# Storing two bias tables once instead of 128 times, reading them with a mirrored skew, and reading the mirrored tile backwards on VectorE

## The chip, the cores and the metric

The kernel runs on one core of a Trainium2 chip. The metric is the device time of one execution in microseconds (us). The times shown are those of three runs of the kernel before the change: 1046.44, 1047.62 and 1049.24 us, median 1047.62.

## What is computed

One layer of a hybrid decoder trunk on 512 tokens with 1024 features, in float32: a SwiGLU half-step, two kinds of attention side by side, their output projection, a second SwiGLU half-step, and a gated embedding. The change touches only how the relative-position bias of the attention reaches the softmax. Cut to that:

```python
def swiglu(x, w_gu, w_down):                 # 1024 -> 2 x 2816 -> 1024
    g, u = jnp.split(x @ w_gu, 2, axis=-1)
    return (jax.nn.silu(g) * u) @ w_down

def banded_attention(q, k, v, rel_bias, max_dist, stride):
    logits = einsum(q, k) * dh ** -0.5
    rel = query index - key index
    bias = rel_bias[t5_bucket(rel * stride)]         # one value per head and distance
    logits = where(0 <= rel <= max_dist, logits + bias, -1e30)
    m = max(logits); pr = exp(logits - m); s = sum(pr); o = pr @ v
    return o, m, s

h = h + 0.5 * rms(swiglu(rms(h), ffn1_w_gu, ffn1_w_down))
z = rms(h) @ w_in + b_in
out_a = sink_swa_gqa(...)       # 8 query heads, 2 key heads, window 128, a sink logit per head
out_b = dilated_mixture(...)    # 8 heads, (window, dilation) in (128,1), (512,4), (2048,16)
h = h + rms(concat(out_a, out_b) @ w_out + b_out)
h = h + 0.5 * rms(swiglu(rms(h), ffn2_w_gu, ffn2_w_down))
h = h + rms(sigmoid(rms(h) @ w_gate) * (p @ w_ple))
```

The bias depends on the head and on the distance between query and key alone. So a head's whole bias is a vector over distances, and the tile that is added to 128 queries by 512 keys is that vector, shifted by one element from one query to the next.

## The kernel before, in words

Every weight matrix is cut into tiles of 128 x 1024 values. A tile goes through the same steps each time (`prep`, L121): SyncE issues a DMA of 512 KB from DRAM into one of three raw buffers (L131), ScalarE casts it to float32r into a ring slot (L132), VectorE subtracts the cast from the raw values into the slot's second half (L133; on GpSimd in the attention), and TensorE multiplies with both halves, three products for each. `release` frees a slot when its last matmul is written down, and `pump` then starts the next tile. All DMAs of the kernel are issued by SyncE, in one order (queue "SPq"); an issue that waits holds all behind it.

The first SwiGLU walks over 22 slices of 128 features (`ffn`, L349). Each slice takes two weight tiles (gate and up, "gu"), 48 matmuls, a Silu on ScalarE (L250), a product on VectorE (L251) and a split into two halves (L252, L253). After slice 6 it calls `tables` (L402).

`tables` makes the bias vectors. Four small matmuls pick the bucket of each distance for 8 heads (L414), four VectorE adds put in the mask (L417). The result lies on 8 partitions of the buffer `FB`, 640 values for the dilated heads and 384 for the windowed ones. Then two DMAs (L421) store it in DRAM tiles `tbb` (8 x 128 x 640) and `tba` (8 x 128 x 384): each head's vector is written 128 times, by a step of 0 on the reading side. The same regions of `FB` are later taken for the three loads of the residual stream `x` that end the first SwiGLU (`load_h`, L198 to L200), which therefore wait for the two stores.

In the attention `load_tab` (L523) reads two heads' tables into SBUF, 128 partitions x 2 heads x 512 (or 256) values. Partition p reads copy p at an offset that goes down by one element from copy to copy (a step of 639 between rows of 640), so partition p holds the vector shifted by p, longest distance first.

`qk_b` (L580) and `qk_a` (L654) compute the logits of a head in four parts by query tile, and a custom VectorE instruction adds the table's slice to the logits in PSUM and takes the row's minimum of the negated, scaled sum (L595 and L674, followed by a short read of the accumulator). ScalarE exponentiates, VectorE scales (L601, L685), TensorE transposes and multiplies by V. Between the heads TensorE is given parts of the input and output projections to fill its time (`filling`, L754).

What matters of order: TensorE's order is the program's; the other engines' and SyncE's order is set by a scheduler that simulates the program, so a shorter DMA can change the order of SyncE's queue.

Of the kernel before, what the change touches and what calls it, by code (L numbers as in the profile page):

```python
# [30 lines left out]


def bias_constants():
    """Per table: which bucket each column (a distance, longest first) takes, times 8, and what is added."""
    b = _buckets(512)
    out = []
    for n, far in ((640, 511), (384, 255)):
        pick = np.zeros((32, n), np.float32)
        add = np.full((8, n), MASKED, np.float32)
        for r in range(n):  # L40
            d = far - r
            if n == 640:
                c = int(0 <= d <= 128) + int(d >= 0 and d % 4 == 0) + int(d >= 0 and d % 16 == 0)
            else:
                c = int(0 <= d <= 127)
            if c:
                pick[b[d], r] = 8.0
                add[:, r] = 8.0 * math.log(c)
        out += [pick, add]
    return out  # L50
# [3 lines left out]
def hybrid_layer(ctx: ExitStack, tc: tile.TileContext, x, p, rel_bias, ffn1_pre_g, ffn1_w_gu, ffn1_w_down,  # L54
# [28 lines left out]

    hd = tc.dram_tile([S, D], F32, name="hd")
    ed = tc.dram_tile([S, D], F32, name="ed")
    tbb = tc.dram_tile([8, P, 640], F32, name="tbb")
    tba = tc.dram_tile([8, P, 384], F32, name="tba")

    make_identity(nc, ident)
    nc.vector.memset(neghalf, -0.5)  # L90
# [10 lines left out]

    ring = [(WR[:, 2 * i, :], WR[:, 2 * i + 1, :]) for i in range(4)]

    # ---- weights: raw from DRAM, then the part that float32r holds and what is left of it
    W = {}
    state = {"raw": 0, "lo": nc.vector}

# [43 lines left out]
        return slot[0][:, k * P:(k + 1) * P], slot[1][:, k * P:(k + 1) * P]  # L151

    def wstat(o, slot, k, cols, start, stop):
        """o += W[k-th rows].T @ xT[k, cols]"""
        wh, wl = kview(slot, k)
        mm(o, wh, XH[:, k, cols], start, False)
        mm(o, wh, XL[:, k, cols], False, False)
        mm(o, wl, XH[:, k, cols], False, stop)

    def xstat(outs, ah, al, wh, wl, start, stop):  # L160
        """outs[n] += a.T @ W[:, n-th 512 columns]"""
        n = len(outs)
        for i in range(n):
            mm(outs[i], ah, wh[:, i * 512:(i + 1) * 512], start, False)
        for i in range(n):
            mm(outs[i], ah, wl[:, i * 512:(i + 1) * 512], False, False)
        for i in range(n):
            mm(outs[i], al, wh[:, i * 512:(i + 1) * 512], False, stop)
# [4 lines left out]
    def flat(a):  # L173
        return a.rearrange("p a b -> p (a b)")

    # ---- norms, one tile of 128 tokens at a time
    cnt = {"h": 0, "x": 0, "s": 0}

    def buf(kind):
# [8 lines left out]
        return small[:, i:i + 1]  # L188

    def rstd(src, junk, half):  # L190
        """1/sqrt(mean of squares + eps), halved if half"""
        ms, r = col(), col()
        nc.scalar.activation(junk, src, AF.Square, scale=1.0 / (16.0 if half else 32.0), accum_out=ms)  # L193
        nc.gpsimd.tensor_scalar(ms, ms, 4 * EPS if half else EPS, None, op0=ALU.add)  # L194
        nc.gpsimd.tensor_tensor(r, ms, neghalf, op=ALU.pow)
        return r
# [10 lines left out]
        return xs  # L207

    def post(t, f, gain, half, y, junk):
        """h + post-norm of f; y takes f * gain"""  # L210
        h = load_h(t, x if state.get("first") else None)
        with tc.high_priority():
            r = rstd(f, junk, half)
            nc.vector.tensor_tensor(y, f, gain, op=ALU.mult)
            nc.vector.scalar_tensor_tensor(h, y, r, h, op0=ALU.mult, op1=ALU.add)
        return h
# [17 lines left out]
        nc.sync.dma_start(BC[:, i, :n], dram(vec, off, [[0, P], [1, n]]))  # L234
        return BC[:, i, :n]

    # ---- SwiGLU
    def gu_half(ffn, ff, slot, cols):
        ps = slot2(slot)
        for i, kind in enumerate("gu"):  # L240
# [22 lines left out]
    halfA, halfB, full = slice(0, 256), slice(256, 512), slice(0, 512)  # L263
    HEAD_FF = 3

    # ---- order of the weights through the ring
    todo += [("ple", 0), ("ple", 1)]

    def gu_list(ffn):
# [1 line left out]

    todo += gu_list("1") + [("d1", k) for k in range(NFF)]

    # ---- start: e = p @ W_ple, first norms
    ring_more = [(ht(7), 11), (ht(8), 13), (ht(9), 15), (ht(10), 17)]
    free.extend(a for a, _ in ring_more[:3])
    praw = FB[:, 6144:7168].rearrange("p (k t c) -> p k t c", k=2, t=NT)
# [69 lines left out]
    release(("ple", 1))  # L347

    def ffn(n, wait_tr, after_first, extra_slots):  # L349
        """wait_tr(t): emits the transposition of token tile t"""  # L350
        wait_tr(0)
        wait_tr(1)
        for ff in range(HEAD_FF):
            gu_half(n, ff, gu_slot(ff), halfA)
            if ff < 2:
                wait_tr(2 + ff)
        for ff in range(NFF):
            s = gu_slot(ff)
            for slot, until in extra_slots:
                if ff == until:  # L360
                    retired.append(slot)
                    free[:] = [a for a in free if a is not slot]
            gu_half(n, ff, s, halfB if ff < HEAD_FF else full)
            gu_evac(n, ff, s)
            release(("u" + n, ff))
            if ff == 6:
                after_first()

    def down(n, extra, finish, between):
        """k-streaming, then the last tiles token tile by token tile; finish(t) follows token tile t."""  # L370
        last = NFF - M_LAST
        for k in range(last):
            for t in range(NT):
                down_part(n, t, k, t, W[("d" + n, k)])
            if k == last - 4:
                free.extend([ht(0), ht(1)])
                retired.extend([free[-1], free[-2]])
            release(("d" + n, k))
        extra()
        for t in range(NT):  # L380
            for k in range(last, NFF):
                if k == NFF - 2 and t >= 2:
                    between(t)
                down_part(n, t, k, t, W[("d" + n, k)])
            if t == NT - 1:
                for k in range(last, NFF):
                    release(("d" + n, k))
            finish(t)
# [11 lines left out]
        nc.vector.tensor_scalar(nsink, psink, -1.0, None, op0=ALU.mult)  # L400

    def tables(slot, slot_after):  # L402
        """the bias rows of every head by distance, and the biases by feature"""
        ps = slot2(slot)
        nc.tensor.transpose(PS[:, 2 * slot_after, 0:18], br, ident[:18, :18])
        nc.vector.tensor_copy(bfeat, PS[:, 2 * slot_after, 0:18])
        jobs = []
        for n, pick, add, h0, dst, base in tabs:
            pk, ab = FB[0:32, base:base + n], (base + 640 if n == 384 else 4352)
            ad = FB[0:8, ab:ab + n]  # L410
            for c in range(0, n, 512):
                w = min(512, n - c)
                o = ps[0:8, 0, 0:w] if w == 512 else (ps[0:8, 1, 0:w] if w == 128 else ps[0:8, 1, 128:128 + w])
                mm(o, rb[:, h0:h0 + 8], pk[:, c:c + w], True, True)  # L414
                jobs.append((ad[:, c:c + w], o))
        for a, o in jobs:
            nc.vector.tensor_tensor(a, a, o, op=ALU.add)  # L417
        for n, pick, add, h0, dst, base in tabs:
            ab = base + 640 if n == 384 else 4352
            ad = FB[0:8, ab:ab + n]  # L420
            nc.sync.dma_start(dst, bass.AP(tensor=ad.tensor, offset=ad.offset, ap=[ad.ap[0], [0, P], [1, n]]))  # L421

    def tr_first(t):
        if t >= 2:
# [26 lines left out]
    down("1", first_extra, finish1, between_parts)  # L451
    state["first"] = False

    # ---- attention
    state["lo"] = nc.gpsimd

    def first(fn):
# [65 lines left out]
    def load_tab(s):  # L523
        if s < 4:
            nc.sync.dma_start(tab(s).rearrange("p (h c) -> p h c", h=2),
                              dram(tbb, 2 * s * P * 640 + 127, [[639, P], [P * 640, 2], [1, 512]]))
        else:
            nc.sync.dma_start(tab(s).rearrange("p (h c) -> p h c", h=2),
                              dram(tba, 2 * (s - 4) * P * 384 + 127, [[383, P], [P * 384, 2], [1, 256]]))

    def z_mm(f, bank, k0, k1):
        for k in range(k0, k1):
# [39 lines left out]

    OFFB = [0, 128, 384, 768]

    def stats(n):
        i = cnt.setdefault("st", 0)
        cnt["st"] += 1
        return small[:, 32 + (i % 8) * 4:32 + (i % 8) * 4 + n]

    def qk_b(s, j):  # L580
# [10 lines left out]
        for i in range(NT):  # L591
            o = (PS[:, 3, 0:256], PS[:, 3, 256:512], PS[:, 4, 0:384], PS[:, 5, :])[i]
            n = (i + 1) * P
            pi = Pm[:, OFFB[i]:OFFB[i] + n]
            nc.vector.tensor_tensor_reduce(out=pi, in0=o[:, :n], in1=tb[:, 384 - i * P:512], scale=-0.125,  # L595
                                           scalar=3.0e38, op0=ALU.add, op1=ALU.min, accum_out=nm[:, i:i + 1])
            nc.scalar.activation(pi, pi, AF.Exp, bias=nm[:, i:i + 1], scale=-1.0, accum_out=rs[:, i:i + 1])
        nc.vector.reciprocal(rs, rs)
# [49 lines left out]
        nc.scalar.copy(hi, v)  # L648
        nc.vector.tensor_tensor(lo, v, f32(hi), op=ALU.subtract)  # L649

    # blocks (query tile, key tile) of the windowed heads
    BLK = [(0, 0), (1, 0), (1, 1), (2, 1), (2, 2), (3, 2), (3, 3)]

    def qk_a(s, j):  # L654
# [15 lines left out]
        for i in range(NT):  # L670
            n = 128 if i == 0 else 256
            c = 0 if i == 0 else i * 256 - 128
            pi = Pm[:, c:c + n]
            nc.vector.tensor_tensor_reduce(out=pi, in0=sview(i)[:, :n], in1=tb[:, 256 - n:256], scale=-0.125,  # L674
                                           scalar=nsink[:, h:h + 1], op0=ALU.add, op1=ALU.min,
                                           accum_out=nm[:, i:i + 1])
            nc.scalar.activation(pi, pi, AF.Exp, bias=nm[:, i:i + 1], scale=-1.0, accum_out=rs[:, i:i + 1])
# [147 lines left out]
    pv_a(7)  # L825
    fill()

    # ---- output projection
    state["lo"] = nc.vector
    todo.extend(gu_list("2") + [("d2", k) for k in range(NFF)])  # L830
    free.extend(a for a, _ in ring_more[2:])
# [27 lines left out]

    ffn("2", tr_second, lambda: None, ring_more)  # L860

    # ---- second SwiGLU's end and the gate
    g_post = bcast(0, ffn2_post_g)
    g_pre = bcast(1, ple_pre_g)

# [88 lines left out]
```

## Time and profile before

| | |
|---|---|
| three runs | 1046.44, 1047.62, 1049.24 us |
| profiled execution, first to last instruction (span) | 1044.5 us |
| the profiled execution's own device time | not listed apart from its span; the median run is 3.1 us above the span |
| TensorE busy | 997.8 us (96%), 4889 matmuls |
| VectorE, ScalarE, GpSimd busy | 449.2, 377.8, 83.2 us |
| mean granted TensorE clock | 0.983 of full speed |
| DMA | 127.58 MB, all but a little of it in one queue |

The profile gives busy time by engine, granted clock and DMA traffic in stretches of the span, the chain of waits that ended last, instructions in order of time with the idle time before each and what ended it, and groups of like instructions with their mean duration. A busy share of TensorE of 96% leaves 47 us of the span idle; the rows below say where. In the timelines a row of SPq shows the time in which SyncE was issuing a DMA, not the time of the transfer.

### The profile page before, as it was taken

To read this page: it belongs to the slowest core of one execution; us is meant where nothing else is said; L and a number is where in the kernel's file an instruction comes from. 1 tells how busy PE (TensorE), PEld (TensorE's weight loads), DVE (VectorE), ACT (ScalarE), POOL (GpSimd) and SP (SyncE) were. 2 spreads that over 40 slices of the span, in tenths; PEclk is the share of its full clock that TensorE was granted. 3 is DMA by queue.
4 is the path that set the end of the run, shared out by engine and by line. 5 is a ranking of instruction groups with operands and counts; after the bars stand their busy time and mean duration, and the time that the engine had idled before them with its cause. 6 is when DMAs were issued, how large, how long until landed. Compare 5 with 4: busy or idle time off the path is not lost.

```text
span 1044.5 us, 12202 instructions
## 1 busy us (share of the span) xinstructions
PE 997.8 (96%) x4889; PEld 841.7 (81%) x4889; DVE 449.2 (43%) x656; ACT 377.8 (36%) x590; POOL 83.2 (8%) x90
## 2 busy tenths in 40 slices
PE   9999991699999999999998999999999999999997
PEld 8987881588888888888887789888888888888886
DVE  5534200542332235647779775533322332223655
ACT  7532100432222224357778544333222322122531
POOL 2000000000000001032223130000000000000211
PEclk9999996799999999999999999999999999999999
DMA  9843545742332344444322356533322223334431
GB/s 316 257 129 103 69 51 65 217 121 61 101 122 88 114 150 152 141 122 136 106 72 92 97 174 214 149 93 101 101 81 61 81 81 121 101 110 169 176 130 61
DMA packets 131747, 127.58 MB, mean 122 GB/s; under 512 B 4361, under 2 KB 111939, under 8 KB 131691
## 3 DMA queue, kind: packets, MB, share of 16 engines
q1 hardware_dynamic: 131691, 126.81, 40.5%
q8 instruction: 38, 0.62, 0.2%
q14 instruction: 18, 0.15, 0.0%
HBM read 109.49 MB, written 14.68 MB: 119 GB/s over the span
## 4 chain that ended last, share of the span: by engine, by line
PE 84%; another core or an unknown queue 7%; DVE 4%; issue 2%; ACT 2%; DMA 1%; POOL 0%; DVEq 0%; SPq 0%; POOLq 0%; ACTq 0%
PE banks L93 82%; DVE hb L649 1%; PE banks L224 1%; DVE hb L545 1%; DVE fb L685 1%; ACT hb L543 0%; DMA fb<-in_p_dram 0%; DVE fb L674 0%; ACT hb L552 0%; DVE hb L727 0%; PE banks L694 0%; ACT wr L132 0%; PE banks L612 0%; DMA raw<-in_w_out_dram 0%
## 5 line engine op out<-in xcount | busy, mean ns | idle before, releaser
L93 PE MATMUL banks<-xh,wr 128*128 128x512 f32 (+1 forms) x1152 | 339.9, 375 | 29.6 <-ACT wr L132 29.5
L93 PEld LDWEIGHTS banks<-xh,wr 128*128 128x128 f32 x1152 | 211.3, 189 | 68.5 <-ACT wr L132 30.0
L93 PE MATMUL banks<-wr,hb 128*128 128x512 f32 x1104 | 255.5, 390 | 0.2 <-DVE hb L727 0.2
L132 ACT CAST wr<-raw 128x1024 fp32r<-128x1024 f32 x114 | 119.8, 1053 | 372.9 <-PE banks L93 278.9
L93 PEld LDWEIGHTS banks<-wr,hb 128*128 128x128 f32 x1104 | 206.4, 188 | 43.1 <-DVE hb L727 0.6
L133 DVE TENSOR_TENSOR wr<-raw,wr 128x1024 fp32r<-128x1024 f32 x100 | 122.1, 1223 | 259.9 <-ACT wr L132 257.8
L93 PE MATMUL banks<-xl,wr 128*128 128x512 f32 (+1 forms) x576 | 214.7, 373 | 0.0
L93 PE MATMUL banks<-xh,hb 128*128 128x512 f32 (+1 forms) x672 | 184.8, 359 | 0.0
L93 PEld LDWEIGHTS banks<-xh,hb 128*128 128x128 f32 x672 | 120.4, 189 | 18.7
L93 PEld LDWEIGHTS banks<-xl,wr 128*128 128x128 f32 x576 | 109.2, 190 | 18.4
L93 PE MATMUL banks<-xl,hb 128*128 128x512 f32 (+1 forms) x336 | 120.5, 359 | 0.0
L132 ACT CAST hb<-raw 128x1024 fp32r<-128x1024 f32 x54 | 56.6, 1052 | 132.1 <-PE banks L93 78.5
L133 DVE TENSOR_TENSOR hb<-raw,hb 128x1024 fp32r<-128x1024 f32 x50 | 61.1, 1224 | 86.0 <-ACT hb L132 85.0
L93 PE MATMUL banks<-hb 128*128 128x512 f32 (+3 forms) x440 | 87.6, 346 | 7.6 <-DVE hb L649 7.1
L93 PEld LDWEIGHTS banks<-hb 128*128 128x128 f32 x440 | 71.6, 190 | 20.8 <-DVE hb L649 10.6
L251 DVE TENSOR_TENSOR fb<-fb,banks 128x512 f32<-128x512 f32 x44 | 30.2, 687 | 131.9 <-PE banks L93 131.2
L194 POOL TENSOR_SCALAR small<-small 128x1 f32<-128x1 f32 x28 | 13.4, 479 | 807.6 <-ACT fb L193 774.4
L93 PEld LDWEIGHTS banks<-xl,hb 128*128 128x128 f32 x336 | 63.5, 189 | 9.3
L133 POOL TENSOR_TENSOR wr<-raw,wr 128x1024 fp32r<-128x1024 f32 x14 | 34.2, 2443 | 96.4 <-ACT wr L132 96.4
L93 PE MATMUL banks<-hb,xh 128*128 128x512 f32 (+1 forms) x172 | 38.6, 374 | 0.0
L93 PEld LDWEIGHTS banks<-hb,xh 128*128 128x128 f32 x172 | 30.9, 188 | 5.9
L252 ACT CAST hb<-fb 128x512 fp32r<-128x512 f32 x44 | 27.3, 620 | 18.0 <-DVE fb L251 18.0
(102 smaller groups left out, 624.7 us busy)
## 6 DMA issues: line engine op xcount, KB each, us to landing
raw<-in_ffn_w_gu_dram SPq DMA_DIRECT2D x88, 512.0 KB, 3.8
raw<-in_ffn_w_down_dram SPq DMA_DIRECT2D x44, 512.0 KB, 3.2
raw<-in_w_in_dram SPq DMA_DIRECT2D x18, 512.0 KB, 4.4
hd<-fb SPq DMA_DIRECT2D x12, 512.0 KB, 2.6
fb<-hd SPq DMA_DIRECT2D x12, 512.0 KB, 3.5
fb<-in_x_dram SPq DMA_DIRECT2D x8, 512.0 KB, 6.5
raw<-in_w_out_dram SPq DMA_DIRECT2D x8, 512.0 KB, 3.3
raw<-in_w_ple_gate_dram SPq DMA_DIRECT2D x8, 512.0 KB, 3.4
```

What stands on the lines that cost most here:

```text
L93: nc.tensor.matmul(o, l, r, start=start, stop=stop)
L132: nc.scalar.copy(hi, raw)
L133: state["lo"].tensor_tensor(lo, raw, f32(hi), op=ALU.subtract)
L194: nc.gpsimd.tensor_scalar(ms, ms, 4 * EPS if half else EPS, None, op0=ALU.add)
L224: nc.tensor.transpose(ps[:, k // 4, (k % 4) * P:(k % 4 + 1) * P], xs[:, k * P:(k + 1) * P], ident)
L251: nc.vector.tensor_tensor(sg, sg, ps[:, 1, :], op=ALU.mult)
L252: nc.scalar.copy(HB[:, 0, ff, :], sg)
L545: nc.vector.scalar_tensor_tensor(q[OWN[1 - j], j, :], PS[OWN[j], bank, :], bfeat[OWN[j], f:f + 1], f32(q[OWN[j], j, :]), op0=ALU.add, op1= ...
L649: nc.vector.tensor_tensor(lo, v, f32(hi), op=ALU.subtract)
L685: nc.vector.tensor_scalar(pi, pi, rs[:, i:i + 1], None, op0=ALU.mult)
```

## The change

Three edits that belong together. The host's tables run from the shortest distance to the longest (with 127 masked values ahead) instead of the other way. The DRAM tiles lose their dimension of 128, so that each head's vector is stored once. `load_tab` reads it with a step of 1 from partition to partition, so that the tile in SBUF is the mirror image of the one before; and the VectorE instruction takes its second operand with a step of -1 from the slice's last element (`back`), which mirrors it again.

```diff
-    for n, far in ((640, 511), (384, 255)):
+    for n in (640, 384):
...
-            d = far - r
+            d = r - 127 if r < n - 1 else -1
...
-    tbb = tc.dram_tile([8, P, 640], F32, name="tbb")
-    tba = tc.dram_tile([8, P, 384], F32, name="tba")
+    tbb = tc.dram_tile([8, 640], F32, name="tbb")
+    tba = tc.dram_tile([8, 384], F32, name="tba")
...
-            nc.sync.dma_start(dst, bass.AP(tensor=ad.tensor, offset=ad.offset, ap=[ad.ap[0], [0, P], [1, n]]))
+            nc.sync.dma_start(dst, ad)
...
-                              dram(tbb, 2 * s * P * 640 + 127, [[639, P], [P * 640, 2], [1, 512]]))
+                              dram(tbb, 2 * s * 640, [[1, P], [640, 2], [1, 512]]))
...
-                              dram(tba, 2 * (s - 4) * P * 384 + 127, [[383, P], [P * 384, 2], [1, 256]]))
+                              dram(tba, 2 * (s - 4) * 384, [[1, P], [384, 2], [1, 256]]))
...
+    def back(a, c0, c1):
+        v = a[:, c0:c1]
+        return bass.AP(tensor=v.tensor, offset=v.offset + c1 - c0 - 1, ap=[v.ap[0], [-1, c1 - c0]])
...
-            nc.vector.tensor_tensor_reduce(out=pi, in0=o[:, :n], in1=tb[:, 384 - i * P:512], scale=-0.125,
+            nc.vector.tensor_tensor_reduce(out=pi, in0=o[:, :n], in1=back(tb, 0, (i + 1) * P), scale=-0.125,
...
-            nc.vector.tensor_tensor_reduce(out=pi, in0=sview(i)[:, :n], in1=tb[:, 256 - n:256], scale=-0.125,
+            nc.vector.tensor_tensor_reduce(out=pi, in0=sview(i)[:, :n], in1=back(tb, 0, n), scale=-0.125,
```

Every engine has as many instructions as before, and TensorE, VectorE, ScalarE and GpSimd have them in the same order. SyncE's queue changes in one place, in the first SwiGLU behind slice 6. Here it is as a piece of the difference (`in_ffn_w_gu` is a gate or up weight tile, `in_x` the residual stream for the end of the first SwiGLU; L421 are the two stores):

```order
 L131 DMA raw<-in_ffn_w_gu_dram 128x8x128
-L421 DMA tbb<-fb 1024x1x640
-L421 DMA tba<-fb 1024x1x384
-L131 DMA raw<-in_ffn_w_gu_dram 128x8x128
-L200 DMA fb<-in_x_dram 128x1024
-L131 DMA raw<-in_ffn_w_gu_dram 128x8x128
-L200 DMA fb<-in_x_dram 128x1024
-L131 DMA raw<-in_ffn_w_gu_dram 128x8x128 x17
+L421 DMA tbb<-fb 8x640
+L421 DMA tba<-fb 8x384
+L200 DMA fb<-in_x_dram 128x1024 x2
+L131 DMA raw<-in_ffn_w_gu_dram 128x8x128 x19
```

The two stores are smaller, and the two loads of `x` that wait for the stores have moved ahead of two weight tiles. The same place in SyncE's queue with the change, with the semaphores that each issue waits for (DMAHW1 and DMAHW2 tell that the store of `tbb` and that of `tba` have landed; DVE and PE are VectorE's and TensorE's progress):

```order
L131 DMA raw<-in_ffn_w_gu_dram 128x8x128 [waits DMAHW4_49,DVE_49]
L421 DMA tbb<-fb 8x640 [waits DVE_49]
L421 DMA tba<-fb 8x384 [waits DVE_49]
L200 DMA fb<-in_x_dram 128x1024 [waits DMAHW1_49,PE_49]
L200 DMA fb<-in_x_dram 128x1024 [waits DMAHW2_49]
L131 DMA raw<-in_ffn_w_gu_dram 128x8x128 [waits DMAHW5_49,DVE_49]
```

All weight tiles behind this place now stand behind the landing of both stores.

## Rows read from the trace of the kernel before

**Rows 1.** Chain of waits, 95 to 200 us: start us, us, what.

```profile
119.61 70.53 another core or an unknown queue
```

**Rows 2.** Busy time by engine, granted clock and DMA in stretches of 5 us.

```profile
core 0: us, PE busy (x) PEld busy (x) DVE busy (x) ACT busy (x) POOL busy (x), PEclk, DMA share, GB/s
155.00:160.00 5.00, 5.00 (x23) 4.13 (x23) 0.00 (x0) 0.00 (x0) 0.00 (x0) 1.00 0.46 51
...
175.00:180.00 5.00, 0.00 (x0) 0.00 (x0) 0.00 (x0) 0.00 (x0) 0.00 (x0) 0.50 0.46 52
...
190.00:195.00 5.00, 3.65 (x8) 2.44 (x9) 2.47 (x3) 3.10 (x4) 0.00 (x0) 0.50 0.96 301
```

**Rows 3.** TensorE's timeline: start us, us, instruction, count, [idle before <-releaser].

```profile
161.38 0.39 PE L93 MATMUL banks<-xh,wr 128*128 128x512 f32 x1
191.32 0.79 PE L93 MATMUL banks<-xh,wr 128*128 128x512 f32 x1 [29.55 <-ACT wr L132]
...
196.31 0.62 PE L93 MATMUL banks<-xh,wr 128*128 128x512 f32 x2
...
214.68 0.62 PE L93 MATMUL banks<-xh,hb 128*128 128x512 f32 x2
```

**Rows 4.** ScalarE's timeline.

```profile
118.06 1.05 ACT L132 CAST wr<-raw 128x1024 fp32r<-128x1024 f32 x1 [3.80 <-PE banks L93]
...
190.22 1.04 ACT L132 CAST wr<-raw 128x1024 fp32r<-128x1024 f32 x1 [70.61 <-DMA raw<-in_ffn_w_gu_dram]
```

**Rows 5.** SyncE's timeline of DMA issues.

```profile
102.71 0.37 SPq L131 DMA_DIRECT2D raw<-in_ffn_w_gu_dram  x1
...
104.37 19.42 SPq L421 DMA_DIRECT2D tba<-fb  x1
123.89 44.16 SPq L131 DMA_DIRECT2D raw<-in_ffn_w_gu_dram  x1
```

**Rows 6.** DMA issues: transfer, count, KB each, median us from issue to landing.

```profile
out_dram<-fb SPq DMA_DIRECT2D x8, 256.0 KB, 2.0
...
fb<-tba SPq DMA_DIRECT2D x4, 256.0 KB, 2.6
...
bc<-in_b_in_dram SPq DMA_DIRECT2D x1, 256.0 KB, 8.4
...
fb<-in_rel_bias_dram SPq DMA_DIRECT2D x1, 2.0 KB, 7.6
```

**Rows 7.** Groups of VectorE instructions, 450 to 592 us: count | busy us, mean ns.

```profile
L674 DVE CUSTOM_DVE_ANT_0 fb<-banks,fb,nsink 128x256 f32<-128x256 f32 x24 | 10.4, 478 | 0.0
...
L595 DVE CUSTOM_DVE_ANT_0 fb<-banks,fb 128x512 f32<-128x512 f32 x8 | 5.5, 685 | 0.0
...
L601 DVE TENSOR_SCALAR fb<-fb,small 128x512 f32<-128x512 f32 x8 | 3.8, 481 | 0.0
...
L601 DVE TENSOR_SCALAR fb<-fb,small 128x128 f32<-128x128 f32 x8 | 2.3, 288 | 0.3
...
L595 DVE CUSTOM_DVE_ANT_0 fb<-banks,fb 128x128 f32<-128x128 f32 x8 | 2.3, 283 | 0.1
```

**Rows 8.** Busy time by engine: dilated heads (450 to 540), windowed heads (534 to 592).

```profile
450.00:540.00 90.00, 89.24 (x469) 74.97 (x468) 61.09 (x163) 62.15 (x131) 25.94 (x12) 1.00 0.39 112
534.00:592.00 58.00, 51.03 (x299) 44.23 (x299) 49.89 (x140) 42.79 (x105) 17.23 (x7) 0.97 0.25 82
```

**Rows 9.** SyncE's issue of the third windowed table.

```profile
542.06 0.38 SPq L528 DMA_DIRECT2D fb<-tba  x1
```

**Rows 10.** VectorE's timeline: first instruction that reads that table.

```profile
560.08 0.35 DVE L674 CUSTOM_DVE_ANT_0 fb<-banks,fb,nsink 128x128 f32<-128x128 f32 x1
```

**Rows 11.** TensorE's timeline in the windowed heads: matmuls with idle time before them.

```profile
558.70 1.82 PE L93 MATMUL banks<-hb 128*128 128x256 f32 x13 [2.01 <-DVE hb L649]
...
584.64 1.07 PE L93 MATMUL banks<-hb 128*128 128x256 f32 x5 [2.17 <-DVE hb L649]
```

**Rows 12.** Busy time and granted clock, 584 to 588 us.

```profile
584.00:588.00 4.00, 3.36 (x15) 3.24 (x16) 3.05 (x9) 1.55 (x2) 0.00 (x0) 0.64 0.44 129
```

## The prediction, made before the change was run

> **What bounds the kernel now.** Start with the shares of busy time: TensorE is busy for 997.8 of 1044.5 us, so there are only 47 us in which another engine or a transfer can be the cause of anything. Next read the chain of waits for a long piece that is not TensorE's. There is one: 70.53 us from 119.61 on stand against an unknown queue [rows 1]. [...]
>
> [...] ScalarE's cast of a weight tile waits for 70.61 us for one tile's DMA [rows 4]. [...] The two stores write 8 heads x 128 copies x (640 + 384) values x 4 bytes = 4.19 MB. At 51 GB/s that is 82 us from 103.5 on, to about 186, which is where the weights begin to arrive again. And TensorE starts a matmul at 161.38, and the next at 191.32, after 29.55 us of idle time that the cast at L132 ended [rows 3, 4]. So this stall comes from the two stores alone.
>
> **The change part by part.**
>
> *The stores shrink.* From 4.19 MB to 8 x 1024 x 4 = 32.8 KB. What they cost TensorE is read from its timeline. Between 196.31 and 214.68 lie 81 matmuls, so one comes every 0.227 us at full clock; behind the one at 161.38 the next was due at 161.61 and came at 191.32: 29.71 us. Then 11 matmuls take from 191.32 to 196.31, 4.99 us, where 11 x 0.227 = 2.50 would do: 2.49 us more, at the lower clock of 0.50 [rows 2, 3] and behind the first new tile. Together 32.20 us. Before and behind the stall TensorE works without a gap and bounds the kernel, so all of it moves the end; the other 17 us of its idle time (47 - 30) lie elsewhere and stay.
>
> *The order of SyncE's queue.* Two loads of x now stand ahead of two weight tiles and wait until both stores have landed. How long such a small store takes is not in the trace. By its bytes at 51 GB/s it is 0.6 us for both; the nearest rows are 2.0 us for 256 KB to DRAM and 7.6 us for 2 KB in a crowded queue [rows 6]. I take some 3 us, ends 2 and 8. Neither costs anything: after the last cast that came in time (118.06) TensorE ran on to 161.6, so the stock of prepared and raw tiles covers over 40 us, and the hold is a fifth of it at most. Without this cover every us of it would be one of TensorE's. Loading x earlier moves no buffer that another needs, and the bytes are the same.
>
> *The table loads.* Eight loads, the same shapes and bytes, now from overlapping rows of DRAM. The trace has no such load. The nearest rows are the same load from separate rows, 2.6 us for 256 KB, and a vector read by 128 partitions from one place, 8.4 us for 256 KB [rows 6]. I take 2.6, since the pieces are as long as before, and keep 8.4. Either is hidden: the load with the least room is issued at 542.06 and first read at 560.08 [rows 9, 10], 18.0 us. At 8.4 us the key copies behind it in the queue would land up to 5.8 us later; the program issues them too a head ahead. If that cover failed once, it would be up to 5.8 us.
>
> *VectorE reads backwards.* 64 instructions have their second operand reversed, 17408 elements in all: 8 x (128 + 256 + 384 + 512) in L595 and 8 x (128 + 3 x 256) in L674. Forward, L595 takes 685 ns for 512 and 283 for 128, so 402/384 = 1.05 ns an element; the scaling at L601 takes (481 - 288)/384 = 0.50 ns [rows 7]. [...] I take 0 us. Bounds: nothing below, as the count is the same; above, no row has a backward read, and the largest step between rates that rows 7 shows is two, so 1.05 ns more for each, 18.3 us in all. Of these the windowed heads' 7168 elements, 7.5 us, would be on the path, since there VectorE is busy 49.89 of 58 us and TensorE waits for it; the dilated heads' 10240, 10.8 us, have 28.9 us of idle VectorE beside them under a TensorE that is 99% busy [rows 8].
>
> [...]
>
> *Host tables, matmuls and adds of `tables`.* Same counts and sizes: nothing.
>
> **The sum.** 1044.5 - 29.71 - 2.49 = 1012.3 us of span. The profiled execution's own time is not listed apart from its span; the median of the runs, 1047.62, is 3.1 us above it, so I put 3.1 us around the new span too: **1015.4 us**.
>
> **The rivals.**
>
> *Backward reads run at half the rate.* For: no row shows one, and VectorE is on the chain in the windowed heads. [...] Time: 1015.4 + 7.5 = 1022.9; with the dilated heads exposed as well 1033.7. [...]
>
> *Overlapping table rows are slow.* All partitions read the same few KB. For: 8.4 us for a broadcast of the same size. Against: 18 us of room. Time: one missed cover, 1015.4 + 5.8 = 1021.2.
>
> *The stores still hold the queue.* If the slowness was in how few partitions they read and not in their bytes, little would change: 1047.6. Against: 4.19 MB at 51 GB/s ends where the stall ends. [...]
>
> *Slower than before: backward reads at a much lower rate.* The same place as the first rival, but far dearer. To eat the 32.2 us and 3.1 more, 17408 elements must each cost 35.3 us / 17408 = 2.0 ns more with everything exposed (2.9 times the forward rate), or, with the 28.9 us idle in the dilated heads used up first, 64.2/17408 = 3.7 ns more (4.5 times). At five times the extra is 73 us less 28.9, so 1059.6. For: nothing but that the read is unknown. [...]
>
> **How the numbers follow.** The likeliest case gets 0.82, half rate 0.10, slow table rows 0.04, stores that still hold the queue 0.02, a much slower backward read 0.02. A measurement of this kernel can tell about 0.3% (3 us) from no change. So faster 0.96, same 0.02, slower 0.02.
>
> The range: the runs before spread from 1.2 below to 1.6 us above their median. And the clock dips once in the windowed heads: TensorE's gaps there reach 2.01 and 2.17 us, and behind the second the granted clock was 0.64 in 584 to 588 [rows 11, 12], 1.4 us of those four lost. When all comes 32 us earlier, that dip may be spared or others may join it: 1.4 less, or two more, some 3 us. So from 1015.4 - 2.9 to 1015.4 + 4.6, about 1012.5 to 1020.0; to take in most of the slow table rows I stretch the top to 1021. What lies outside are the half-rate case and the two last ones, 0.14.
>
> **What would show each step right or wrong.** In the changed profile: no idle time of TensorE over 1 us between 100 and 260 us, no granted clock below 1.00 there, no cast of a gate or up tile that waits for a DMA for more than a few us; SyncE's issue of the second store under 2 us; the x loads issued before 115 us. L595 at 685 ns for 512 and L674 at 478 for 256 as before; a longer one proves the first rival, and its factor decides between the first and the last. Table loads at 2.6 and 3 to 4 us; more proves the second. The prediction is wrong if TensorE shows a new gap in the first SwiGLU, or if the attention between its first head and the output projection takes over 3 us longer than before.

## The result, and the profile after

The changed kernel took 1017.37 us (median of 4 runs, 1016.05 to 1017.71) beside 1048.43 us for the kernel before (4 runs, 1046.44 to 1049.33): a ratio of 0.9701, 95% interval 0.9687 to 0.9715. That is 31.1 us less; 1015.4 us was predicted.

The stretches of 5 us that answer to [rows 2] show TensorE at work, the clock at 1.00, and ScalarE going on with the weights in both, VectorE in the first; in [rows 2] those two did nothing in either, with 51 and 52 GB/s on the DMA engines, and TensorE nothing in the second, at a clock of 0.50:

```profile
155.00:160.00 5.00, 5.00 (x24) 4.14 (x23) 1.23 (x1) 1.47 (x2) 0.00 (x0) 1.00 0.30 90
175.00:180.00 5.00, 5.00 (x24) 4.14 (x23) 0.00 (x0) 0.60 (x1) 0.00 (x0) 1.00 0.33 98
```

SyncE's queue at the stores (as [rows 5]): each store is issued in 0.3 us where the second took 19.42 and the weight tile behind it 44.16, the two loads of x go out together 3.3 us after the second store's issue began (by then both landings have been waited for), and the weights follow:

```profile
107.73 0.30 SPq L421 DMA_DIRECT2D tbb<-fb  x1
108.20 0.29 SPq L421 DMA_DIRECT2D tba<-fb  x1
111.47 0.84 SPq L200 DMA_DIRECT2D fb<-in_x_dram  x2
113.74 16.69 SPq L131 DMA_DIRECT2D raw<-in_ffn_w_gu_dram  x4
```

The weights of the first SwiGLU come in time again. ScalarE's casts (as [rows 4]) follow each other every 5.4 us, and what ends the idle time before each is TensorE freeing a slot, not a DMA:

```profile
122.28 1.05 ACT L132 CAST wr<-raw 128x1024 fp32r<-128x1024 f32 x1 [3.80 <-PE banks L93]
...
127.72 1.05 ACT L132 CAST wr<-raw 128x1024 fp32r<-128x1024 f32 x1 [3.89 <-PE banks L93]
```

VectorE's custom instruction, now reading its table backwards (the groups that answer to the first, second and last of [rows 7]; its lines are 4 higher in the changed file):

```profile
L678 DVE CUSTOM_DVE_ANT_0 fb<-banks,fb,nsink 128x256 f32<-128x256 f32 x24 | 10.5, 479 | 0.0
...
L599 DVE CUSTOM_DVE_ANT_0 fb<-banks,fb 128x512 f32<-128x512 f32 x8 | 5.5, 685 | 0.0
...
L599 DVE CUSTOM_DVE_ANT_0 fb<-banks,fb 128x128 f32<-128x128 f32 x8 | 2.3, 283 | 0.1
```

Forward it took 478, 685 and 283 ns. A step of -1 cost nothing here. The loads of the windowed tables, now from overlapping source rows, took longer than the 2.6 us of before [rows 6]:

```profile
fb<-tba SPq DMA_DIRECT2D x4, 256.0 KB, 3.5
```

3.5 us is inside the 18 us of room: the third windowed table is issued at 514.08 and first read at 532.09.

Where the time went can be followed with one landmark, the matmul behind the 2.01 us gap in the windowed heads [rows 11], and one start mark, VectorE's first add of `tables` (the traces have three such adds, not four). TensorE's row in the changed kernel:

```profile
530.72 1.82 PE L93 MATMUL banks<-hb 128*128 128x256 f32 x13 [2.01 <-DVE hb L653]
```

The landmark moved from 558.70 to 530.72, 27.98 us earlier. But the start mark moved the other way. First the kernel before, then the changed kernel, VectorE's timeline:

```profile
100.87 0.68 DVE L417 TENSOR_TENSOR fb<-fb,banks 8x512 f32<-8x512 f32 x1 [0.27 <-PE banks L93]
```

```profile
105.09 0.68 DVE L417 TENSOR_TENSOR fb<-fb,banks 8x512 f32<-8x512 f32 x1 [0.27 <-PE banks L93]
```

This execution was 4.22 us late before it reached anything that the change touches, so between the two marks it gained 27.98 + 4.22 = 32.20 us.

### The profile page after: what moved, and what is told of

It reads as the page before. It is cut to its first block, busy times and chain, and to the rows that moved or that the text cites. A ratio compares the mean times of both kernels' runs of the same rounds, so it can differ in the third digit from the quotient of the medians.

```text
span 1015.4 us, 12202 instructions
## 1 busy us (share of the span) xinstructions
PE 996.4 (98%) x4889; PEld 840.8 (83%) x4889; DVE 449.7 (44%) x656; ACT 377.8 (37%) x590; POOL 82.0 (8%) x90
## 4 chain that ended last, share of the span: by engine, by line
PE 90%; DVE 5%; ACT 2%; issue 2%; DMA 1%; DVEq 0%; POOL 0%; SPq 0%; POOLq 0%; ACTq 0%
PE banks L93 88%; DVE hb L653 2%; PE banks L224 1%; DVE hb L545 1%; DMA fb<-in_p_dram 1%; DVE fb L689 1%; DVE fb L678 1%; ACT hb L543 0%; ACT hb L552 0%; DVE hb L731 0%; PE banks L616 0%; DVE hb L554 0%; DMA hb<-hb 0%; ACT fb L724 0%; ACT wr L132 0%
## 5 line engine op out<-in xcount | busy, mean ns | idle before, releaser
L93 PE MATMUL banks<-hb 128*128 128x512 f32 (+3 forms) x440 | 86.7, 344 | 7.6 <-DVE hb L653 7.1
L194 POOL TENSOR_SCALAR small<-small 128x1 f32<-128x1 f32 x28 | 12.1, 432 | 779.7 <-ACT fb L193 747.3
```

The source lines that it names most:

```text
L93: nc.tensor.matmul(o, l, r, start=start, stop=stop)
```

## The experiments

Eight runs were made: seven further kernels, and the changed kernel once more. Their comparisons share the runs of the kernel before: 13 for the first four (median 1048.27), 19 for the last four (1047.76).

### The backward read alone

```diff
-            nc.sync.dma_start(dst, ad)
+            nc.sync.dma_start(dst, bass.AP(tensor=ad.tensor, offset=ad.offset, ap=[ad.ap[0], [0, P], [1, n]]))
-                              dram(tbb, 2 * s * 640, [[1, P], [640, 2], [1, 512]]))
+                              dram(tbb, 2 * s * P * 640, [[641, P], [P * 640, 2], [1, 512]]))
...
```

(against the changed kernel; `tba` and the two DRAM tiles likewise)

> The mirrored host tables and the backward VectorE read of the change, but with 128 copies stored as before (partition p reads copy p one element further, a step of 641). Theory A (all of the gain is in the stores' bytes; a backward read costs nothing): the time of the kernel before, 1048.4, within 0.3%, with TensorE's stall of about 30 us in the first SwiGLU and the custom VectorE instruction at 685 ns for 512 elements. Theory B (the backward read or the mirrored tables give some of the 31 us): 1 us or more below the kernel before. Theory C (the backward read costs some us that the stores' gain hid): 3 us or more above it.

Measured: 1046.77 us (10 runs), ratio 0.9988, interval 0.9977 to 0.9999. TensorE's stall is there, and the instruction takes what it takes forward:

```profile
191.44 0.79 PE L93 MATMUL banks<-xh,wr 128*128 128x512 f32 x1 [29.47 <-ACT wr L132]
```

```profile
L599 DVE CUSTOM_DVE_ANT_0 fb<-banks,fb 128x512 f32<-128x512 f32 x8 | 5.5, 686 | 0.0
```

Theory C falls, and the stores carry the gain. The median is 1.5 us lower, which meets theory B's wording (1 us or more) as well as theory A's (within 0.3%), and the interval all but reaches no change. The trace decides between them, by the two marks:

```profile
101.08 0.68 DVE L417 TENSOR_TENSOR fb<-fb,banks 8x512 f32<-8x512 f32 x1 [0.27 <-PE banks L93]
```

```profile
558.74 1.82 PE L93 MATMUL banks<-hb 128*128 128x256 f32 x13 [2.03 <-DVE hb L653]
```

From the start mark to the landmark this kernel took 457.66 us, the kernel before 457.83; from the start mark to the end of the span 943.8 us, the kernel before 943.6. So the profiled execution saved nothing behind its start, and theory B gets nothing from it. Where the median's 1.5 us came from stays open.

### 96 copies, 64 copies

```diff
-    tbb = tc.dram_tile([8, 640], F32, name="tbb")
+    tbb = tc.dram_tile([8, 96, 640], F32, name="tbb")
-            nc.sync.dma_start(dst, ad)
+            nc.sync.dma_start(dst, bass.AP(tensor=ad.tensor, offset=ad.offset, ap=[ad.ap[0], [0, 96], [1, n]]))
...
```

(against the changed kernel; the loads read the first copy; 64 likewise)

> The changed kernel, but each table is stored 96 times (only the first copy is read). Theory A (the store moves about 51 GB/s and holds the weights behind it; TensorE has some 43 us of prepared weights from the last cast in time): before, 128 copies took 86.7 us from the store's issue (103.5) to the first cast behind it (190.2); 96 copies take 65 us, so that the next matmul starts at 169.6 instead of 161.6: a stall of 8 us and 2.5 us at the lower clock, 1017.4 + 10.5 = 1028. Theory B (the time goes with the copies, no cover): 1017.4 + 0.75 x 31 = 1041. Theory C (what slows the queue is that the store reads 8 partitions with a step of 0, whatever its length): 1048.

Measured: 1027.25 us (4 runs), ratio 0.9801, interval 0.9781 to 0.9820. From ScalarE's and TensorE's timelines:

```profile
171.29 1.04 ACT L132 CAST wr<-raw 128x1024 fp32r<-128x1024 f32 x1 [51.34 <-DMA raw<-in_ffn_w_gu_dram]
```

```profile
172.39 0.79 PE L93 MATMUL banks<-xh,wr 128*128 128x512 f32 x1 [10.27 <-ACT wr L132]
```

> The changed kernel, but each table is stored 64 times. Theory A (51 GB/s, cover of some 43 us from the last cast in time, 58 us from the store's issue): 43 us from the store's issue to the next cast, before the stock is used up: no stall, the time of the changed kernel, 1017.4, though the queue is held for 41 us. Theory B (the time goes with the copies): 1033. Theory C (the layout, not the bytes): 1048.

Measured: 1016.76 us (4 runs), ratio 0.9699, interval 0.9677 to 0.9720. TensorE has no gap, although ScalarE waited for a weight tile for 30.66 us:

```profile
151.31 1.05 ACT L132 CAST wr<-raw 128x1024 fp32r<-128x1024 f32 x1 [30.66 <-DMA raw<-in_ffn_w_gu_dram]
```

For 64 copies it came out as theory A said. For 96 the time did, 1027.25 for 1028, but the parts were larger than theory A had them. The gap was 10.27 us instead of 8, and from the start mark (101.22) to the landmark (540.35) this kernel took 13.50 us longer than the changed one, where theory A had 10.5. The rest, some 3 us, lies behind the gap, where the granted clock was 0.50 from 170 to 175 us and 0.67 from 175 to 180. The medians do not show this sharply, since that of the changed kernel itself moves: with 96 copies the time is 9.9 us above the first median of that kernel and 12.1 above its second (below).

From the first store's issue to the next cast it was 46.8 us for 64 copies (104.55 to 151.31), 67.4 for 96 (103.86 to 171.29) and 86.7 for 128, so some 20 us for each 32 copies. TensorE's time is not lost in proportion: with 64 copies it lost none, and from 96 to 128 the cast came 19.28 us later and TensorE's gap was 19.28 us longer (29.55 for 10.27), with the lower clock of 0.50 on top. Half of the copies would have given the whole gain.

### The same bytes from 128 partitions

```diff
-            nc.sync.dma_start(dst, bass.AP(tensor=ad.tensor, offset=ad.offset, ap=[ad.ap[0], [0, P], [1, n]]))
+            full = FB[:, ab:ab + n]
+            nc.sync.dma_start(bass.AP(tensor=dst.tensor, offset=dst.offset, ap=[[8 * n, P], [n, 8], [1, n]]),
+                              bass.AP(tensor=full.tensor, offset=full.offset, ap=[full.ap[0], [0, 8], [1, n]]))
```

(against the kernel before, as the rest below)

> The kernel before, with the same 4.19 MB stored in the same two DRAM tiles, but read from all 128 partitions, each row 8 times, instead of from 8 partitions, each row 128 times. The rows of the other partitions hold other data, so the tables are not the reference's. Theory A1 (the bytes are slow because they come from 8 partitions): the stores move at 150 GB/s or more, under 28 us, within TensorE's cover: no stall, 1016 to 1020. Theory A2 (4.19 MB of such a store is slow from wherever it is read, by its rows of 2.5 and 1.5 KB with a step of 0 or by its writes): 51 GB/s and the stall again, 1048.

Measured: 1016.00 us (4 runs), ratio 0.9687, interval 0.9663 to 0.9712. The stretch behind the stores' issue:

```profile
110.00:115.00 5.00, 5.00 (x24) 4.14 (x23) 1.57 (x2) 1.64 (x2) 0.00 (x0) 1.00 1.04 405
```

405 GB/s instead of 51 (stores and weights together), and no stall. So 4.19 MB in 128 copies are not slow as such. This run changes two things at once, the partitions that are read and the share of the DMA engines that is busy (1.04 in this stretch, stores and weights, beside 0.46); the last run keeps that share.

### The changed kernel again

> The changed kernel once more, unaltered, for the spread of its start. In its first profile the tables were made at 105.09 us, in the kernel before at 100.87, and in the four kernels of the first experiments, whose programs are the same up to there, at 101.1 to 101.9. Theory A (the start scatters by execution, about 4 us of the span, and has nothing to do with the change): tables at 101 to 102 this time, a span near 1012, which is what the sum gave. Theory B (the change delays the start): tables at 105 again, a span of 1015.

Measured: 1015.18 us (4 runs, 1014.51 to 1018.47), ratio 0.9702, interval 0.9682 to 0.9723. VectorE's and TensorE's timelines:

```profile
100.53 0.67 DVE L417 TENSOR_TENSOR fb<-fb,banks 8x512 f32<-8x512 f32 x1 [0.27 <-PE banks L93]
```

```profile
526.16 2.09 PE L93 MATMUL banks<-hb 128*128 128x256 f32 x13 [2.03 <-DVE hb L653]
```

Theory A: the start scatters. The landmark lies 558.70 - 526.16 = 32.54 us before that of the kernel before, the start mark 0.34 us before: 32.20 us between the two marks, the same as in the first profile. The other three kernels without the stall agree: between the marks it was 425.61 us with 64 copies, 425.60 with 128 partitions and 425.62 with partitions apart (below), beside 425.63 in both profiles of the changed kernel and 457.83 before. The span was 1013.8 and not 1012, for a reason behind the landmark: this execution had two dips of the clock in the windowed heads, where the kernel before had one [rows 12].

```profile
528.00:532.00 4.00, 4.00 (x18) 3.58 (x17) 3.37 (x9) 3.40 (x12) 0.00 (x0) 0.64 0.00 0
...
556.00:560.00 4.00, 4.00 (x17) 3.21 (x16) 2.79 (x4) 1.38 (x2) 0.00 (x0) 0.72 0.00 0
```

### The wait for the landing taken away

```diff
-            ab = base + 640 if n == 384 else 4352
+            ab = 1024 if n == 384 else 0
...
```

> The kernel before, with the table's vectors at another place of the buffer (regions that the last loads of x don't take), so that no issue on SyncE's queue waits for the stores to land; 128 copies in the same queue. Theory A1 (the weights stand behind the stores' rows in the DMA rings): the stall as before, 1047 to 1049. Theory A2 (the x loads' wait for the landing holds SyncE): no stall or a short one, 1017 to 1030.

Measured: 1048.08 us (10 runs), ratio 1.0005, interval 0.9994 to 1.0016. The three loads of x now all go out ahead of the stores (in the kernel before one did, at 101.08, and two waited), no load of x waits for a store to land, and the stall is as it was:

```profile
194.06 0.80 PE L93 MATMUL banks<-xh,wr 128*128 128x512 f32 x1 [29.20 <-ACT wr L132]
```

The time is theory A1's, and theory A2 falls: the x loads' wait for the stores, and with it the order of SyncE's queue that the change also altered, had no part in the stall. What holds the weights behind the stores, this run does not show.

### The stores in GpSimd's queue

```diff
-            ab = base + 640 if n == 384 else 4352
+            ab = 1024 if n == 384 else 0
-            nc.sync.dma_start(dst, bass.AP(tensor=ad.tensor, offset=ad.offset, ap=[ad.ap[0], [0, P], [1, n]]))
+            nc.gpsimd.dma_start(dst, bass.AP(tensor=ad.tensor, offset=ad.offset, ap=[ad.ap[0], [0, P], [1, n]]))
...
```

> As the kernel with the moved source, and the two stores of 128 copies are issued by GpSimd instead of SyncE, so they have rings of their own. Theory A1 (what holds the weights is only their place behind the stores in one ring): the weights pass the stores, no stall, 1016 to 1021. Theory A2 (the stores fill the DMA engines themselves, whichever ring they come from; 8 of the 16 engines are busy with them, and every weight tile uses all 16): a weight tile takes several times its 3.8 us for some 80 us, the stall stays in part or whole, 1030 to 1048.

Measured: 1048.91 us (10 runs), ratio 1.0010, interval 0.9991 to 1.0030. TensorE's timeline has two gaps in place of one, with some 8 us of work between them:

```profile
167.75 0.79 PE L93 MATMUL banks<-xh,wr 128*128 128x512 f32 x1 [8.26 <-ACT fb L250]
192.96 0.79 PE L93 MATMUL banks<-xh,wr 128*128 128x512 f32 x1 [16.89 <-ACT wr L132]
```

The view of DMA queues from 110 to 185 us (packets, MB, share of 16 engines; the first is GpSimd's queue), and the weights' median time from issue to landing:

```profile
q0 software_dynamic: 1345, 4.00, 84.2%
q1 hardware_dynamic: 2467, 1.59, 6.8%
...
raw<-in_ffn_w_gu_dram SPq DMA_DIRECT2D x3, 512.0 KB, 75.5
```

The time is theory A2's. The weights have a queue to themselves, but only three tiles come in 75 us, while the stores' packets keep the DMA engines busy from the other queue. So a queue of its own does not free the weights. One thing is not as theory A2 had it. The stores' packets took 84.2% of the 16 engines' time here, not half of it, where the kernel before shows a busy share of 0.46 [rows 2]; and they moved 4.00 MB in 75 us, which is 53 GB/s, no more than before. Nearly twice the engines' time for the same rate speaks against the engines as what set the rate, which the next run tests. It also means that this run does not tell what held the weights in the kernel before: the 0.46 of the engines' time that the stores took, or the weights' place behind the stores in one queue.

### Eight partitions further apart

```diff
-            nc.sync.dma_start(dst, bass.AP(tensor=ad.tensor, offset=ad.offset, ap=[ad.ap[0], [0, P], [1, n]]))
+            far = FB[0:32:4, ab:ab + n]
+            nc.sync.dma_start(dst, bass.AP(tensor=far.tensor, offset=far.offset, ap=[far.ap[0], [0, P], [1, n]]))
```

> The kernel before, with the stores' 8 rows read from partitions 0, 4, 8 to 28 instead of 0 to 7; 128 copies of each, the same bytes and as many rows, partitions and DMA engines. The rows of these partitions hold other data, so the tables are not the reference's. [...] Theory E (8 rows keep 8 DMA engines busy at 6 GB/s each, wherever they lie): 51 GB/s, the stall as before, 1048.

Measured: 1017.33 us (4 runs), ratio 0.9716, interval 0.9696 to 0.9737. While the stores run:

```profile
115.00:120.00 5.00, 5.00 (x24) 4.14 (x23) 2.05 (x3) 1.20 (x3) 0.00 (x0) 1.00 0.52 207
```

207 GB/s at a busy share of 0.52, where partitions 0 to 7 gave 51 at 0.46 [rows 2]. As many rows, bytes and copies, about the same share of the engines, and four times the rate: theory E, 51 GB/s wherever the rows lie, falls. So the stores were slow because they read 4.19 MB from 8 neighbouring partitions; why neighbours give a quarter of the rate, no run shows.

No other kernel beat the changed one: the kernels without the stall lie between 1015.2 and 1017.4 us, which is the spread of one kernel, and the four others are slower.

## Why the prediction was right

**The stall's size.** 29.71 us of idle time and 2.49 us behind it, 32.20 in all, came out of two profiles of the changed kernel to the second decimal between the two marks, and of three other kernels without the stall within 0.03 us. That the whole of it would move the end was argued from TensorE being the bound on both sides; it is shown now up to the landmark, and behind it the rest of the span was 484.7, 485.8 and 487.6 us (changed kernel, kernel before, changed kernel again) with none, one and two dips of the clock. What ties the stall to the stores is [rows 2], 51 GB/s before TensorE ran dry and 52 while it stood, and the length of SyncE's issues: 19.42 us for the second store and 44.16 for the next weight tile before, 6.27 and 9.90 with the partitions apart, 0.29 for the second store in the changed kernel. What makes an issue last so long is not shown.

**The hidden parts.** The wait of the x loads behind both stores was taken as 3 us with ends of 2 and 8: it was 3.3. The cover for it was put at over 40 us, counted from the last cast that came in time. Behind that cast ScalarE waited 30.66 us for a tile with 64 copies, which cost TensorE nothing, and 51.34 us with 96, which cost a gap of 10.27 us: so the cover was some 41 us. The table loads were taken as 2.6 us and were 3.5, below the bound of 8.4, and hidden. By the prediction's own sign (more than 2.6 proves the second rival) that rival's premise came true, and its cost, a missed cover, did not.

**The backward read.** That it would add 0 us was the author's estimate, since no row of the kernel before has a backward read; the runs showed 479, 685 and 283 ns, where forward it was 478, 685 and 283, so it added nothing. The rivals that hung on it have no support left.

**Where the sum was loose.** The forecast was 2.0 us below the first median and 0.2 us above the second; the second is that close by luck, since the start and the clock's dips alone move an execution by more. Its last term, 3.1 us around the span, was misnamed: in nearly all runs that list both, the time is 1.8 us above the span (1017.18 and 1015.4 for the profiled one; 2.4 at most), and the other 1.3 us was that the profiled execution of the kernel before, by this estimate at some 1046.3 us, was faster than the median run. So the sum aimed at the median after all, and for the profiled execution alone it would have been 1014.1. What moved one profiled execution of the same kernel against another was the start, which the range did not name, and the clock's dips, which it did. The first add of `tables` came at 100.53 to 105.09 us in the profiles. Of dips in the windowed heads there was none in the first profile of the changed kernel, two in the second, one before. And the range's lower end, 2.9 us below, is more than its two terms give: 1.2 and 1.4 make 2.6.

**The rival that the stores still hold the queue** was dismissed because the bytes set the time. That is right for the change, but only half of what the runs show: the bytes set the time at a rate, 51 GB/s, that the eight neighbouring partitions set. All 128 copies cost TensorE nothing when they were read from partitions further apart, at 207 GB/s; a kernel that puts the right vectors there was not run.

## What to carry to other kernels

A transfer off the critical path cost nothing here while the stock of what queues behind it lasted (64 copies, a cast that waited 30.66 us, no gap), and everything after that (from 96 copies to 128, 19.28 us more of waiting and 19.28 of gap): look for a stretch in which the DMA rate is far below the usual one while the engines still work, and compare its length with that stock. The store that repeats eight neighbouring partitions 128 times was such a transfer, at 51 GB/s; write fewer bytes (1017.37 us here), or read them from partitions that lie apart (207 GB/s, 1017.33 us); GpSimd's queue in place of SyncE's did not help here (1048.91 us). And compare two profiles between marks on both sides of the change, because a start that scatters by 4 us hides or feigns more than a tenth of a gain like this one.

## What the runs showed that I had not expected

The start scatters by more than the runs' spread had led me to think. The chain of waits at the start of the kernel before and of the changed kernel (start us, us, what):

```profile
1.76 4.67 DMA fb<-in_p_dram
...
7.13 8.20 PE banks L93 x36
```

```profile
1.76 6.44 DMA fb<-in_p_dram
...
9.36 10.26 PE banks L93 x36
```

One of the first loads (of `p`, issued at 1.76 us) takes 1.8 us longer, and the 36 matmuls behind it 10.26 us instead of 8.20. Both programs are the same up to there; what sets it was not tried. The other two profiles whose chain has this load at over 6 us start late too (6.21 and 6.31 us; first add at 103.96 and 104.03).

The stores from eight neighbouring partitions moved 51 GB/s, those from eight that lie four apart 207, and a separate queue for the slow stores left the weights about as late as before: 75.5 us for a tile, where the median in the kernel before is 3.8.

Loads whose 128 rows overlap in DRAM took longer where they were expected to cost the same. For the windowed tables (256 KB) they took 3.2 to 4.7 us in the four profiles with overlapping rows, and 2.6 to 2.8 in the six with rows apart, the mirrored tables of the backward read alone among them (2.8). Why it was 4.1 and 4.7 with 96 and 64 copies and 3.5 and 3.2 with one is open.
